# 64-wide turns by identity products become 128-wide transposes in a chunked recurrence, its outputs are formed beside its states, and attention scores use all 128 rows

## The chip, the cores and the metric

The kernel runs on one core of a Trainium2 chip. TensorE (PE in the rows) multiplies and transposes into eight PSUM banks of 128 x 512 f32; VectorE (DVE) and ScalarE (ACT) read the banks; GpSimd (POOL) does a few small things; loads are issued on the sync engine's queue (SP). The metric is device time of one execution in microseconds, lower is better.

## What is computed

Two transformer-like blocks over 512 tokens of width 1024. The change touches the first block's recurrence and the scores of the attention in both blocks.

```python
def rwkv7_step(state, inp):                       # 8 heads of 64, 512 steps
    r_t, w_t, k_t, v_t, a_t, b_t = inp
    sa = jnp.einsum('bhij,bhj->bhi', state, a_t)
    state = state * w_t[:, :, None, :] + sa[..., None] * b_t[:, :, None, :] + v_t[..., None] * k_t[:, :, None, :]
    y = jnp.einsum('bhij,bhj->bhi', state, r_t)
    return state, y
...
    y = yc * lax.rsqrt(jnp.mean(yc * yc, axis=-1, keepdims=True) + GN_EPS)
    y = y.reshape(b_, s_, D_RWKV) * lnx_g.astype(f32) + lnx_b.astype(f32)
...
    s = jnp.einsum('bhnqd,bhnkd->bhnqk', qc, kb).astype(jnp.float32) * (HEAD_DIM ** -0.5)   # band attention, 8 heads
...
        s = jnp.einsum('bhqd,bhkd->bhqk', qi, kh).astype(f32) * scale                       # second block, 4 heads
```

The first block projects the normalized input, runs the recurrence (512 channels) and a banded attention (512 channels), gates both and projects back. The second block has a state-space mixer, a second attention and a convolution side by side, and then 32 experts of which each token uses two. All in f32; large products are split into a high and a low part in f32r (one pass on TensorE), small ones are f32 (two passes).

## The kernel before

**Tiling of the recurrence.** Channels lie on partitions, so two heads of 64 fill 128 partitions (`HS` are the two halves), and there are four head pairs. The 512 steps are cut into chunks of 64; `rwkv_unit` treats one pair and one half of the sequence, four chunks (`NC = 4`), so there are 8 units. Two lanes of two pairs each run interleaved, with the attention (`att_stream`) and the modulation products (`ada_stream`) beside them.

**A unit, in order.** `pz` and `pa` are two small projections. `AR` holds the scaled a and r vectors, `BK` the scaled b and k. `psc` multiplies BK by AR for each chunk and head, masked into `SB[h]`. Then come the turns, which bring tokens to the partitions: `ptk` (BK into `SB[h][:, :, 128:192]`, by transposes of 64 rows), `pat` (the a part of AR into `RH`) and `pvt` (v into `UV`), both by products with the identity, 64 x 64, for each chunk and head, followed by one copy for each head. `pav` multiplies SB by UV. A triangular inverse of 32-wide blocks follows (`pf`, `p1`, `p2`), then `pwu`, `pgq` (into `Gb` and `Qb`) and `ph` (state parts `H_`). The state chain runs over the chunks (`px`, one product and one vector operation at a time). Then `py` forms the outputs: for each chunk `Qb` times the state, and SB times UV for each head, on the same bank. They are normalized over the head, turned back (`pyt`, again by identity products), scaled by `lnx_g` and `lnx_b`, and gated into `y`.

**Scores.** `score_parts` splits q and k: `Q[h]` holds the high part of q on one half of the partitions and the low part on the other, `K[h]` the high part of k twice, and `L` the low part of k. `scores` adds two f32r products on one bank: one with 128 rows, and one with 64 rows for L. It is called 32 times in the first block and 16 times in the second.

**What sets the order.** Nothing is issued as it is written. A recorder notes all operations; a planner (`schedule`, `cost`, `best`) then chooses, by a list of priorities and its own costs, an order for each engine, the PSUM bank of each tile and, for operations that are offered in two forms (`flex`, `copy`), ACT or DVE. It charges 130 ns when TensorE's tile shape changes and prefers to stay with a shape; all products on one PSUM tile keep their written order. `arrange` places the SBUF tiles. The order is then emitted and each engine follows its own list. All instructions are emitted from one line of the file (965), so the rows are told apart by shape.

Of the kernel before, what the change touches and what calls it, by code (L numbers as in the profile page):

```python
# [1012 lines left out]
def trace(R, T, off, dbg=None, stop=None):  # L1013
# [3 lines left out]
    C = {}  # L1017
# [216 lines left out]
    def rps(name):  # L1234
        return mmps(name, "rw", 4)
# [26 lines left out]
    def halves(name):  # L1262

        return rps(name + "0"), rps(name + "1")

    HS = (slice(0, 64), slice(64, 128))
    view = lambda p, n: p[:, :NC * n].rearrange("p (c n) -> p c n", n=n)

    def rwkv_unit(lane, pr, half, kx, kk, vx, rx, gx, st_):
# [34 lines left out]
        R.vector.scalar_tensor_tensor(ath, ath, 1.0, kk, ALU.add, ALU.mult)  # L1304
        AR = t512("AR")
        R.vector.scalar_tensor_tensor(AR[:, :, 0:64], kk, -1.0, E[:, :, 0:64], ALU.mult, ALU.mult)
        R.tt(AR[:, :, 64:128], rx, E[:, :, 1:65], ALU.mult)
        BK = t512("BK")
# [7 lines left out]
        for c in range(NC):  # L1316
            for h, hs in enumerate(HS):
                mm(ps_[h][:, 128 * c:128 * c + 128], lhsT=BK[hs, c], rhs=AR[hs, c], start=True, stop=True)
        SB = (t768("SB0"), t768("SB1"))
# [8 lines left out]
        yield  # L1328
        pt = halves("ptk")
        for c in range(NC):  # L1330
            for h, hs in enumerate(HS):
                R.tensor.transpose(pt[h][:, 64 * c:64 * c + 64], BK[hs, c], C["ident"][hs, hs])
        for h in range(2):
            R.copy(SB[h][:, :, 128:192], view(pt[h], 64))
        R32 = t256("R32")
# [5 lines left out]
        RH = t512("RH")  # L1341
        pt = halves("pat")
        for c in range(NC):
            for h, hs in enumerate(HS):
                mm(pt[h][hs, 64 * c:64 * c + 64], lhsT=AR[hs, c, 0:64], rhs=C["ident"][hs, hs], start=True, stop=True)
        for h, hs in enumerate(HS):
            R.copy(RH[hs, :, 0:64], view(pt[h], 64)[hs])
        UV = t512("UV").rearrange("p c (h n) -> p c h n", h=2)
        yield
        pt = halves("pvt")  # L1350
        for c in range(NC):
            for h, hs in enumerate(HS):
                mm(pt[h][HS[1 - h], 64 * c:64 * c + 64], lhsT=vx[hs, c], rhs=C["ident"][hs, hs], start=True, stop=True)
        for h in range(2):
            R.copy(UV[HS[1 - h], :, h], view(pt[h], 64)[HS[1 - h]])
        yield
# [68 lines left out]
        for h, hs in enumerate(HS):  # L1425
            pv = view(pt[h], 128)[hs]
            R.tt(Gb[hs, :, hs], pv[:, :, 64:128], i2b[hs], ALU.add)
            R.tt(Qb[hs, :, hs], pv[:, :, 0:64], AR[hs, :, 64:128], ALU.add)
        H_ = t256("H")
        p = view(rps("ph"), 64)  # L1430
        for c in range(NC):
            for h, hs in enumerate(HS):
                mm(p[hs, c], lhsT=SB[h][:, c, 128:192], rhs=UV[:, c, h], start=True, stop=True, tile_position=(0, 64 * h))
        R.tt(H_, p, D.unsqueeze(2).to_broadcast([128, NC, 64]), ALU.mult)
# [20 lines left out]
        st_.append(S2)  # L1455
        Y = view(rps("py"), 64)
        for c in range(NC):
            mm(Y[:, c], lhsT=Qb[:, c], rhs=X[:, c], start=True, stop=False)
            for h, hs in enumerate(HS):
                mm(Y[hs, c], lhsT=SB[h][:, c, 64:128], rhs=UV[:, c, h], start=False, stop=True, tile_position=(0, 64 * h))  # L1460

# [23 lines left out]
        yield  # L1485
        pt = halves("pyt")
        yn = t256("yn")
        for c in range(NC):
            for h, hs in enumerate(HS):
                mm(pt[h][hs, 64 * c:64 * c + 64], lhsT=Yc[hs, c], rhs=C["ident"][hs, hs], start=True, stop=True)  # L1490
        for h, hs in enumerate(HS):
            R.vector.tensor_scalar(yn[hs], view(pt[h], 64)[hs], Pc["lnx_g"][hs, c1], Pc["lnx_b"][hs, c1], ALU.mult, ALU.add)
        R.tt(yn, yn, bo, ALU.add)
# [37 lines left out]
    def qk_norm(j, g, name):  # L1531
# [11 lines left out]
        return o  # L1543

    def score_parts(q, k):

        Q, K = ([R.tile([128, 512], F32R, name) for _ in range(2)] for name in ("qs", "ks"))
        L = R.tile([128, 512], F32R, "kl")
        for h, hs in enumerate(HS):
            o = HS[1 - h]  # L1550
            R.copy(Q[h][hs], q[hs])
            R.tt(Q[h][o], q[hs], Q[h][hs].bitcast(F32), ALU.subtract)
            R.copy(K[h][hs], k[hs])
            R.copy(K[h][o], k[hs])
            R.tt(L[hs], k[hs], K[h][hs].bitcast(F32), ALU.subtract)
        return Q, K, L

    def scores(parts, h, qt, n):
        Q, K, L = parts
        ts = slice(128 * qt, 128 * qt + 128)  # L1560
        S = mmps("S")[:, :n]
        R.tensor.matmul(S, lhsT=Q[h][:, ts], rhs=K[h][:, :n], start=True, stop=False)
        R.tensor.matmul(S, lhsT=Q[h][HS[h], ts], rhs=L[HS[h], :n], start=False, stop=True)
        return S
# [1002 lines left out]
```

## Time and profile before

| what | value |
|---|---|
| median of 3 runs | 1463.89 us (1462.17 to 1464.84) |
| the profiled execution | 1457.32 us |
| its span, from first to last instruction | 1455.5 us |
| mean granted TensorE clock | 0.957 |

In the rows below, times are microseconds unless marked ns. The forms are rows*columns of the weights, then the moving operand. PE times are of matmul instructions, whose ends are modelled: the step from one start to the next is a measurement, a busy time less so. An f32 product is two matmul instructions, a transpose or an f32r product one.

### The profile page before, as it was taken

The page shows a single profiled execution, that of the slowest core. Times are in us where ns is not written, and L with a number is a line of the kernel's source. Part 1 is how long each engine was busy: PE and PEld are TensorE (multiplying, and loading weights), DVE is VectorE, ACT ScalarE, POOL GpSimd, SP SyncE. Part 2 cuts the span into 40 slices and gives each one's busy share as a digit, 9 for nine tenths or more (in the row PEclk, how much of TensorE's full clock was granted, in tenths as well). Part 3 has the DMA queues.
Part 4 walks back from the last instruction along what each step waited for, and adds up shares of the span by engine and source line. Part 5 has one row for each costly group of instructions (what it writes and reads, how often), then busy time and mean ns, then how long its engine had stood idle before and what let it go on. Part 6 is the DMA issues. An engine that isn't in the chain of part 4 may idle for free. (4 is left out here: it accounts for less than half of the span.)

```text
span 1455.5 us, 21894 instructions
## 1 busy us (share of the span) xinstructions
PE 1364.7 (94%) x7796; PEld 948.7 (65%) x7796; DVE 1204.1 (83%) x2196; ACT 814.0 (56%) x1250; POOL 167.7 (12%) x125
## 2 busy tenths in 40 slices
PE   5999999998999999999999899999999999989993
PEld 2766666666667787878789666666665565555562
DVE  5595882678796756799975889999999999999985
ACT  5463342455553335346652477877776676657762
POOL 0000000000010000000010213111132011151103
PEclk8999999999988998999999799999999999999997
DMA  9727377010011722000163489999999999999955
GB/s 333 295 93 260 139 238 283 30 38 23 31 44 52 247 81 70 15 30 1 58 232 130 158 297 341 364 368 364 348 362 352 351 344 361 349 337 313 359 188 180
DMA packets 90741, 307.78 MB, mean 211 GB/s; under 512 B 12034, under 2 KB 15490, under 8 KB 89604
## 3 DMA queue, kind: packets, MB, share of 16 engines
q1 hardware_dynamic: 85252, 293.75, 56.3%
q0 software_dynamic: 5376, 12.59, 2.5%
q8 instruction: 62, 1.02, 0.3%
q14 instruction: 51, 0.42, 0.1%
HBM read 293.72 MB, written 18.87 MB: 215 GB/s over the span
## 5 line engine op out<-in xcount | busy, mean ns | idle before, releaser
L965 PE MATMUL ps<-arear 128*80 128x512 f32 (+3 forms) x4435 | 1065.6, 391 | 31.1 <-DVE arear L965 15.8
L965 PEld LDWEIGHTS ps<-arear 128*80 128x80 f32 (+1 forms) x4435 | 704.5, 172 | 325.9 <-DVE arear L965 38.1
L965 ACT ACTIVATE arear<-areaf 128x1024 fp32r<-128x1024 f32 (+5 forms) x536 | 494.2, 949 | 283.7 <-PE ps L965 217.9
L965 DVE TENSOR_TENSOR arear<-areaf,arear 128x1024 fp32r<-128x1024 f32 (+5 forms) x560 | 600.5, 1106 | 61.5 <-ACT arear L965 28.9
L965 PE MATMUL ps<-areaf 64*64 64x64 f32 (+17 forms) x3361 | 371.3, 311 | 37.6 <-DVE areaf L965 26.4
L965 PEld LDWEIGHTS ps<-areaf 128*128 128x128 f32 (+6 forms) x3361 | 256.9, 149 | 158.4 <-issue 56.3
L965 ACT ACTIVATE areaf<-areaf 128x512 f32<-128x512 f32 (+11 forms) x238 | 121.3, 526 | 143.6 <-DVE areaf L965 119.4
L965 ACT ACTIVATE areaf<-ps 128x256 f32<-128x256 f32 (+7 forms) x253 | 110.4, 449 | 136.6 <-PE ps L965 126.5
L957 POOL DMA_INDIRECT yscr<-areaf,areai x32 | 110.3, 3448 | 464.2 <-DVE areaf L965 437.2
L965 DVE TENSOR_TENSOR areaf<-ps,areaf 80x512 f32<-80x512 f32 (+6 forms) x244 | 123.4, 514 | 23.7 <-PE ps L965 22.3
L965 DVE SCALAR_TENSOR_TENSOR areaf<-areaf 128x512 f32<-128x512 f32 (+6 forms) x190 | 108.7, 599 | 23.4 <-ACT areaf L965 17.8
L965 DVE TENSOR_TENSOR areaf<-areaf 128x512 f32<-128x512 f32 (+11 forms) x234 | 100.7, 451 | 8.6 <-ACT areaf L965 4.8
L965 DVE SCALAR_TENSOR_TENSOR areaf<-ps,areaf 128x511 f32<-128x511 f32 (+9 forms) x120 | 57.7, 493 | 41.2 <-PE ps L965 38.6
L965 POOL MEMSET areaf<- 128x512 f32 (+10 forms) x52 | 16.7, 328 | 422.9 <-PE ps L965 178.4
L965 ACT ACTIVATE areaf<-ps,areaf 128x128 f32<-128x128 f32 (+2 forms) x88 | 43.9, 534 | 36.7 <-PE ps L965 30.5
L965 POOL TENSOR_TENSOR areaf<-areaf 128x4 f32<-128x4 f32 (+2 forms) x21 | 20.8, 993 | 359.3 <-DVE areaf L965 328.8
L965 DVE TENSOR_SCALAR areaf<-areaf 128x1 f32<-128x1 f32 (+11 forms) x194 | 46.7, 266 | 14.8 <-PE ps L965 13.3
L965 DVE SCALAR_TENSOR_TENSOR areaf<-areaf,ps 80x512 f32<-80x512 f32 (+1 forms) x72 | 48.7, 676 | 0.8 <-ACT areaf L965 0.7
L965 DVE CAST arear<-areaf 128x1024 fp32r<-128x1024 f32 (+4 forms) x63 | 37.1, 588 | 10.9 <-PE ps L965 10.5
L965 ACT ACT_TABLE_LOAD x35 | 44.9, 1283 | 1.3 <-PEq L2553 0.7
L965 DVE COPY areaf<-ps 32x128 f32<-32x128 f32 (+9 forms) x58 | 22.4, 390 | 20.4 <-ACT areaf L965 14.4
L965 ACT ACTIVATE arear<-ps 128x320 fp32r<-128x320 f32 (+1 forms) x35 | 14.5, 415 | 27.6 <-PE ps L965 27.5
(31 smaller groups left out, 187.9 us busy)
## 6 DMA issues: line engine op xcount, KB each, us to landing
areaf<-in_wx_dram SPq DMA_DIRECT2D x384, 512.0 KB, 5.5
areaf<-in_wada_dram SPq DMA_DIRECT2D x56, 512.0 KB, 5.0
areaf<-in_win_c_dram SPq DMA_DIRECT2D x43, 512.0 KB, 4.4
areaf<-in_wada_dram SPq DMA_DIRECT2D x8, 1024.0 KB, 8.3
areaf<-in_wout_dram SPq DMA_DIRECT2D x16, 512.0 KB, 4.5
areaf<-in_xt_dram SPq DMA_DIRECT2D x16, 256.0 KB, 2.9
yscr<-areaf SPq DMA_DIRECT2D x8, 512.0 KB, 9.4
areaf<-in_win_c_dram SPq DMA_DIRECT2D x24, 128.0 KB, 7.5
```

The source lines that it names most:

```text
L957: self.emitted[i] = self.nc.gpsimd.indirect_dma_start(un(a[0]), bass.IndirectOffsetOnAxis(ap=un(k["idx"]), axis=0), un(k["in_"]), None, bo ...
L965: self.emitted[i] = getattr(getattr(self.nc, eng), op)(*[un(v) for v in a], **{n: un(v) for n, v in k.items()})
```

## The change

It does five things. `pat`, `pvt` and `pyt` become `turned`: 128x128 transposes of two chunks and two heads at a time on one bank, then one copy for each head and each chunk of the two, half of them from one half of the partitions to the other. `ptk` becomes four 128x128 transposes. AR holds its two parts one after the other. The products of SB and UV for the outputs stand beside those for the states, on a bank that the products with Qb are added to after the state chain; the scaling by `lnx_g` and `lnx_b` may go to ACT or DVE, from columns that are also kept with halves exchanged. In the scores, L becomes a tile for each head with zeros in its other half, so that its product has 128 rows.

```diff
--- before.py
+++ after.py
@@ -1265,6 +1265,24 @@
 
     HS = (slice(0, 64), slice(64, 128))
     view = lambda p, n: p[:, :NC * n].rearrange("p (c n) -> p c n", n=n)
+    chunks = lambda t: t.rearrange("p (q g) n -> p q g n", g=2)
+
+
+    lnx = [[Pc[n] for n in ("lnx_g", "lnx_b")], []]
+    for v in lnx[0]:
+        o = R.tile([128, 4], F32, "lnx")
+        for h in range(2):
+            R.copy(o[HS[1 - h]], v[HS[h]])
+        lnx[1].append(o)
+
+    def turned(name, src):
+
+
+        p = rps(name)
+        for q in range(NC // 2):
+            R.tensor.transpose(p[:, 128 * q:128 * q + 128], src[:, 2 * q:2 * q + 2].rearrange("p c n -> p (c n)"), C["ident"])
+        v = p[:, 0:64 * NC].rearrange("p (q h n) -> p q h n", h=2, n=64)
+        return [(h, g, v[HS[g], :, h]) for h in range(2) for g in range(2)]
 
     def rwkv_unit(lane, pr, half, kx, kk, vx, rx, gx, st_):
         t128, t256, t512, t768, ept = lane
@@ -1302,9 +1320,9 @@
         R.vector.tensor_scalar(k2, ath, hka[:, c1], oka[:, c1], ALU.mult, ALU.add)
         R.tt(k2, kx, k2, ALU.mult)
         R.vector.scalar_tensor_tensor(ath, ath, 1.0, kk, ALU.add, ALU.mult)
-        AR = t512("AR")
-        R.vector.scalar_tensor_tensor(AR[:, :, 0:64], kk, -1.0, E[:, :, 0:64], ALU.mult, ALU.mult)
-        R.tt(AR[:, :, 64:128], rx, E[:, :, 1:65], ALU.mult)
+        AR = t512("AR").rearrange("p c (h n) -> p (c h n)", h=2).rearrange("p (h c n) -> p h c n", h=2, n=64)
+        R.vector.scalar_tensor_tensor(AR[:, 0], kk, -1.0, E[:, :, 0:64], ALU.mult, ALU.mult)
+        R.tt(AR[:, 1], rx, E[:, :, 1:65], ALU.mult)
         BK = t512("BK")
         for h, hs in enumerate(HS):
             bs, ks = (HS[h], HS[1 - h])
@@ -1315,7 +1333,7 @@
         ps_ = halves("psc")
         for c in range(NC):
             for h, hs in enumerate(HS):
-                mm(ps_[h][:, 128 * c:128 * c + 128], lhsT=BK[hs, c], rhs=AR[hs, c], start=True, stop=True)
+                mm(ps_[h][:, 128 * c:128 * c + 128], lhsT=BK[hs, c], rhs=AR[hs, :, c], start=True, stop=True)
         SB = (t768("SB0"), t768("SB1"))
         msk = C["m2s"].unsqueeze(1).to_broadcast([128, NC, 128])
         ABc = t128("ABc")
@@ -1326,12 +1344,11 @@
                 R.copy(ABc[q], pv[q, :, 32 * b:32 * b + 32])
             R.tt(SB[h][:, :, 0:128], pv, msk, ALU.mult)
         yield
-        pt = halves("ptk")
+        pt = rps("ptk")
         for c in range(NC):
-            for h, hs in enumerate(HS):
-                R.tensor.transpose(pt[h][:, 64 * c:64 * c + 64], BK[hs, c], C["ident"][hs, hs])
-        for h in range(2):
-            R.copy(SB[h][:, :, 128:192], view(pt[h], 64))
+            R.tensor.transpose(pt[:, 128 * c:128 * c + 128], BK[:, c], C["ident"])
+        for h, hs in enumerate(HS):
+            R.copy(SB[h][:, :, 128:192], view(pt, 128)[:, :, hs])
         R32 = t256("R32")
         R.gpsimd.memset(R32, 0.0)
         for h in range(2):
@@ -1339,20 +1356,12 @@
             R.copy(R32[q, :, 32 * h:32 * h + 32], SB[h][q, :, 32:64])
         yield
         RH = t512("RH")
-        pt = halves("pat")
-        for c in range(NC):
-            for h, hs in enumerate(HS):
-                mm(pt[h][hs, 64 * c:64 * c + 64], lhsT=AR[hs, c, 0:64], rhs=C["ident"][hs, hs], start=True, stop=True)
-        for h, hs in enumerate(HS):
-            R.copy(RH[hs, :, 0:64], view(pt[h], 64)[hs])
+        for h, g, p in turned("pat", AR[:, 0]):
+            R.copy(chunks(RH)[HS[h], :, g, 0:64], p)
         UV = t512("UV").rearrange("p c (h n) -> p c h n", h=2)
         yield
-        pt = halves("pvt")
-        for c in range(NC):
-            for h, hs in enumerate(HS):
-                mm(pt[h][HS[1 - h], 64 * c:64 * c + 64], lhsT=vx[hs, c], rhs=C["ident"][hs, hs], start=True, stop=True)
-        for h in range(2):
-            R.copy(UV[HS[1 - h], :, h], view(pt[h], 64)[HS[1 - h]])
+        for h, g, p in turned("pvt", vx):
+            R.copy(UV.rearrange("p (q g) h n -> p q g h n", g=2)[HS[1 - h], :, g, h], p)
         yield
         pt = halves("pav")
         for c in range(NC):
@@ -1425,12 +1434,14 @@
         for h, hs in enumerate(HS):
             pv = view(pt[h], 128)[hs]
             R.tt(Gb[hs, :, hs], pv[:, :, 64:128], i2b[hs], ALU.add)
-            R.tt(Qb[hs, :, hs], pv[:, :, 0:64], AR[hs, :, 64:128], ALU.add)
+            R.tt(Qb[hs, :, hs], pv[:, :, 0:64], AR[hs, 1], ALU.add)
         H_ = t256("H")
         p = view(rps("ph"), 64)
-        for c in range(NC):
-            for h, hs in enumerate(HS):
-                mm(p[hs, c], lhsT=SB[h][:, c, 128:192], rhs=UV[:, c, h], start=True, stop=True, tile_position=(0, 64 * h))
+        Y = view(rps("py"), 64)
+        for o, whole, w in ((p, True, slice(128, 192)), (Y, False, slice(64, 128))):
+            for c in range(NC):
+                for h, hs in enumerate(HS):
+                    mm(o[hs, c], lhsT=SB[h][:, c, w], rhs=UV[:, c, h], start=whole or c == 0, stop=whole, tile_position=(0, 64 * h))
         R.tt(H_, p, D.unsqueeze(2).to_broadcast([128, NC, 64]), ALU.mult)
         yield
 
@@ -1453,11 +1464,8 @@
             R.vector.scalar_tensor_tensor(o, pt[:, :64], D[:, c:c + 1], H_[:, c], ALU.mult, ALU.add)
             yield
         st_.append(S2)
-        Y = view(rps("py"), 64)
         for c in range(NC):
-            mm(Y[:, c], lhsT=Qb[:, c], rhs=X[:, c], start=True, stop=False)
-            for h, hs in enumerate(HS):
-                mm(Y[hs, c], lhsT=SB[h][:, c, 64:128], rhs=UV[:, c, h], start=False, stop=True, tile_position=(0, 64 * h))
+            mm(Y[:, c], lhsT=Qb[:, c], rhs=X[:, c], start=False, stop=(c == NC - 1))
 
         mu_ = R.tile([128, NC], F32, "gmu")
         R.vector.tensor_reduce(mu_, Y, AX.X, ALU.add)
@@ -1483,13 +1491,12 @@
         R.scalar.activation(gth, gx, AF.Tanh, scale=0.5)
         R.vector.scalar_tensor_tensor(gth, gth, 1.0, gx, ALU.add, ALU.mult)
         yield
-        pt = halves("pyt")
         yn = t256("yn")
-        for c in range(NC):
-            for h, hs in enumerate(HS):
-                mm(pt[h][hs, 64 * c:64 * c + 64], lhsT=Yc[hs, c], rhs=C["ident"][hs, hs], start=True, stop=True)
-        for h, hs in enumerate(HS):
-            R.vector.tensor_scalar(yn[hs], view(pt[h], 64)[hs], Pc["lnx_g"][hs, c1], Pc["lnx_b"][hs, c1], ALU.mult, ALU.add)
+        for h, g, p in turned("pyt", Yc):
+            lg_, lb_ = (lnx[g != h][n][HS[g], c1] for n in range(2))
+            o = chunks(yn)[HS[h], :, g]
+            R.flex(("scalar", "activation", (o, p, AF.Identity), {"scale": lg_, "bias": lb_}),
+                   ("vector", "tensor_scalar", (o, p, lg_, lb_, ALU.mult, ALU.add), {}))
         R.tt(yn, yn, bo, ALU.add)
         R.vector.scalar_tensor_tensor(v3(y[pr][:, ts]), yn, 0.5, gth, ALU.mult, ALU.mult)
 
@@ -1542,17 +1549,20 @@
         R.vector.scalar_tensor_tensor(o, o, g, sq, ALU.mult, ALU.mult)
         return o
 
+    none = R.tile([128, 512], F32, "none")
+    R.gpsimd.memset(none, 0.0)
+
     def score_parts(q, k):
 
-        Q, K = ([R.tile([128, 512], F32R, name) for _ in range(2)] for name in ("qs", "ks"))
-        L = R.tile([128, 512], F32R, "kl")
+        Q, K, L = ([R.tile([128, 512], F32R, name) for _ in range(2)] for name in ("qs", "ks", "kl"))
         for h, hs in enumerate(HS):
             o = HS[1 - h]
             R.copy(Q[h][hs], q[hs])
             R.tt(Q[h][o], q[hs], Q[h][hs].bitcast(F32), ALU.subtract)
             R.copy(K[h][hs], k[hs])
             R.copy(K[h][o], k[hs])
-            R.tt(L[hs], k[hs], K[h][hs].bitcast(F32), ALU.subtract)
+            R.tt(L[h][hs], k[hs], K[h][hs].bitcast(F32), ALU.subtract)
+            R.copy(L[h][o], none[o])
         return Q, K, L
 
     def scores(parts, h, qt, n):
@@ -1560,7 +1570,7 @@
         ts = slice(128 * qt, 128 * qt + 128)
         S = mmps("S")[:, :n]
         R.tensor.matmul(S, lhsT=Q[h][:, ts], rhs=K[h][:, :n], start=True, stop=False)
-        R.tensor.matmul(S, lhsT=Q[h][HS[h], ts], rhs=L[HS[h], :n], start=False, stop=True)
+        R.tensor.matmul(S, lhsT=Q[h][:, ts], rhs=L[h][:, :n], start=False, stop=True)
         return S
 
     def softmax(S, n, bias):
```

## Rows read from the trace of the kernel before

**Rows 1.** The page: busy time, share and instructions; granted clock in 40 slices.
```profile
PE 1364.7 (94%) x7796; PEld 948.7 (65%) x7796; DVE 1204.1 (83%) x2196; ACT 814.0 (56%) x1250; POOL 167.7 (12%) x125
...
PEclk8999999999988998999999799999999999999997
```

**Rows 2.** Stretches: length, busy time of PE, PEld, DVE, ACT, POOL, clock, DMA, GB/s.
```profile
60.00:220.00 160.00, 157.84 (x1295) 102.49 (x1294) 126.67 (x327) 75.07 (x144) 6.21 (x13) 1.00 0.53 179
220.00:300.00 80.00, 80.00 (x464) 55.38 (x464) 36.53 (x82) 23.72 (x41) 3.04 (x7) 0.96 0.37 136
300.00:500.00 200.00, 188.92 (x1506) 134.75 (x1506) 165.74 (x465) 101.59 (x217) 12.15 (x26) 0.91 0.21 66
...
680.00:740.00 60.00, 58.69 (x389) 48.35 (x389) 59.48 (x184) 42.31 (x111) 4.74 (x5) 1.00 0.27 88
...
860.00:1400.00 540.00, 518.15 (x2260) 322.00 (x2259) 526.64 (x571) 383.83 (x432) 107.71 (x30) 0.99 0.96 350
```

**Rows 3.** Waits of PE from 60 to 500 us: total, times, longest.
```profile
PE ps L965 <- DVE areaf L965: 9.2, 19, 1.6
```

**Rows 4.** Timeline of PE at 580 us: start, length, instructions merged.
```profile
579.64 20.75 PE L965 MATMUL ps<-arear 128*128 128x512 f32 x89
```

**Rows 5.** PE instructions by form, 60 to 510 us: count, busy, mean ns, idle before.
```profile
L965 PE MATMUL ps<-areaf 64*64 64x64 f32 x512 | 33.6, 231 | 1.2 <-DVE areaf L965 1.1
...
L965 PE MATMUL ps<-areaf 64*128 64x64 f32 x64 | 7.6, 252 | 0.6 <-ACT areaf L965 0.5 <-DVE areaf L965 0.2
```

**Rows 6.** Timeline of PE around half a turn that stands alone.
```profile
491.63 0.47 PE L965 MATMUL ps<-arear 128*128 128x512 f32 x1
492.03 0.68 PE L965 MATMUL ps<-areaf 64*64 64x64 f32 x8
492.64 0.50 PE L965 MATMUL ps<-arear 128*128 128x512 f32 x1
```

**Rows 7.** Timeline of PE: 128x128 f32 passes between f32r ones; then one alone.
```profile
165.69 0.77 PE L965 MATMUL ps<-areaf 128*128 128x128 f32 x6
166.26 0.71 PE L965 MATMUL ps<-arear 128*128 128x512 f32 x2
166.81 0.27 PE L965 MATMUL ps<-areaf 128*128 128x128 f32 x1
```

**Rows 8.** Timeline of PE: state products; later, a chunk of the outputs.
```profile
208.33 0.69 PE L965 MATMUL ps<-areaf 128*64 128x64 f32 x16
208.95 0.73 PE L965 MATMUL ps<-arear 128*128 128x512 f32 x2
...
294.94 0.70 PE L965 MATMUL ps<-areaf 128*64 128x64 f32 x6
295.45 0.71 PE L965 MATMUL ps<-arear 128*128 128x512 f32 x2
```

**Rows 9.** Timeline of PE: both products of one score, and what follows.
```profile
719.20 0.91 PE L965 MATMUL ps<-arear 128*128 128x512 f32 x2
720.03 1.97 PE L965 MATMUL ps<-areaf 128*128 128x64 f32 x12
```

**Rows 10.** DVE and ACT instructions by form, 60 to 510 us.
```profile
L965 DVE TENSOR_SCALAR areaf<-ps,areaf 64x256 f32<-64x256 f32 x16 | 8.6, 538 | 0.4
L965 DVE COPY areaf<-ps 64x256 f32<-64x256 f32 x10 | 4.2, 420 | 3.8 <-ACT areaf L965 3.4 <-PE ps L965 0.2
...
L965 ACT ACTIVATE areaf<-ps 64x256 f32<-64x256 f32 x54 | 20.4, 377 | 41.9 <-PE ps L965 39.9 <-DVE areaf L965 1.5
L965 ACT ACTIVATE arear<-areaf 64x512 fp32r<-64x512 f32 x15 | 9.4, 629 | 10.5 <-DVE areaf L965 6.1 <-PE ps L965 4.1
L965 ACT ACTIVATE areaf<-ps 32x128 f32<-32x128 f32 x25 | 6.7, 267 | 12.4 <-PE ps L965 10.5 <-DVE areaf L965 1.6
```

**Rows 11.** Stretches of 20 us with a lower granted clock (the share before DMA).
```profile
420.00:440.00 20.00, 18.50 (x134) 12.85 (x136) 17.91 (x46) 9.73 (x19) 1.53 (x2) 0.66 0.05 13
...
460.00:480.00 20.00, 19.65 (x121) 15.31 (x120) 8.74 (x27) 4.00 (x10) 0.00 (x0) 0.66 0.32 106
```

## The prediction, made before the changed kernel was run

> **What bounds the kernel now.** The page comes first: TensorE (PE) is busy for 94% of the span and VectorE (DVE) for 83% [rows 1]. That average covers stages with different limits, so the table of stretches is next [rows 2]. The recurrence, the attention beside it and the modulation products run between about 60 and 500 us (the 64-wide products that only the recurrence issues all lie there). In that stretch PE is busy 157.84 of 160, 80 of 80 and 188.92 of 200 us, DVE 126.67, 36.53 and 165.74. In the second block's attention, 680 to 740 us, DVE is busy 59.48 of 60. In the expert stage, 860 to 1400 us, the DMA engines are busy 96% of the time at 350 GB/s: nothing of the change lies there, and it can only start earlier or later. So a microsecond cut from PE between 60 and 500 us should come off the end, as far as PE is what that stretch waits for.
>
> Is it? The view of waits says yes: in 440 us PE waited longest, in total, for DVE, and only 9.2 us [rows 3]. But the end of a matmul is modelled, so "busy" holds lost time too. The step from one start to the next shows it. At full clock, 512-column passes follow each other at 20.75/89, some 0.23 us [rows 4]. Whatever takes longer than its columns need is where the change can earn. I read those steps in the order of time (timeline).
>
> **The change, part by part.**
>
> *Turns.* Per unit (there are 8: four head pairs, two halves) the products by the identity for pat, pvt and pyt go, 8 each. An f32 product is two passes, so 48 passes of 64x64 go, and 8 transposes of 64 rows (ptk). In come 2+2+2+4 = 10 transposes of 128x128. The 64x64 form has 512 passes with 33.6 us busy; a quarter of them is pav, which stays, so 25.2 us go, and 7.6 us of ptk [rows 5]. Two corrections. A lone half turn of 8 passes reads 0.68 us but the next pass starts after 0.61, so busy overstates by 0.07 per block; and the pass before it took 0.40 instead of 0.23 until the turn began, so entering another tile shape costs 0.17 [rows 6]. With 32 blocks (8 x 4): 32.8 - 2.2 + 5.4 = 36 us if each is entered alone, 31 if none is. The trace has no row that singles out a 128-wide transpose fed from a recurrence tile. The nearest is a run of six 128x128 f32 passes that took 0.57 us to the next start, 0.095 each [rows 7]; from above, the 0.27 us that one such pass is busy in full. So 80 transposes cost 8 to 22 us. I take 8, since they can queue among f32r passes of the same shape. Removed: 31 to 36; net between 9 and 28, and I take 25, near the upper end, as each block was found entered more often than not.
>
> *Outputs beside states.* Y was, for each of 4 chunks, two passes of 128x128 (Qb) and then four of 128x64, all on one bank and thus in that order. One such alternation reads six passes in 0.51 us, plus 0.17 to enter [rows 8]: 0.68 x 4 x 8 = 22 us if each stands alone. After it, the 128x64 passes join those of ph: 16 passes took 0.62 us [rows 8], and 8 passes of Qb at 0.095 need 0.76, so 1.4 x 8 = 11. Between 0 (where chunks were already adjacent) and 11; I take 6. It also moves 16 passes off the end of the state chain; that is worth nothing by itself, for the chain has other work under it. The price is a PSUM bank held from ph to the end of the chain. In exchange ptk, pat, pvt and pyt need one bank where they needed two. I count it as nothing; if a bank were missing, PE would wait for the chain.
>
> *Scores.* The second product had 64 rows, another tile shape. First and second, both of 512 columns, took 0.83 us instead of 2 x 0.23 [rows 9]: 0.37 lost, 48 times, 18 us if each stood alone. Scores of neighbouring heads often stand together, which halves it: 9. Of the 48, 16 lie in the second block's attention, where DVE is full [rows 2]; there PE's gain is worth nothing. That leaves 6; bounds 3 and 12.
>
> *Added on ACT and DVE.* Each turn for pat and pvt is four copies of 64x128 instead of two of 64x256. A 64x256 copy takes 420 ns on DVE and 377 on ACT; the small end is 267 for 32x128 on ACT [rows 10], so the four take about 4 x 270 against 2 x 400: 0.3 us more, 16 times, 5 us. For pyt, two scalings of 538 ns on DVE [rows 10] become four that may also go to ACT. At between 267 and 538 each (I take 340): 0.3 us more, 8 times, 2 us. The zero halves of L are 12 copies of 64x512 at 629 ns [rows 10], or 7.5 us. In sum some 15 us over two engines. ACT is busy for 56% of the span [rows 1], so it is not on the path unless DVE is. The layout of AR and the four lnx copies change nothing that I can price: as many elements as before, and the lnx copies are done once.
>
> **Sum.** PE between 60 and 500 us gets 25 + 6 + 6 = 37 us less work. Does all of it pass? From 60 to 300 us DVE is busy 163 of 240 [rows 2]; half the units lie there, and I let nearly all of 18 us pass: 17. From 300 to 500 us DVE is already at 165.74 of 200. Less PE work would make that 166 plus some 4 of 182, or 93%; engines that feed each other in a fixed order don't both run at that. I let somewhat over half pass: 11. Together 28. The profiled execution took 1457.3 us (span 1455.5), so 1429; the median of the runs shown is 6.6 us above it, so **1436 us**.
>
> The order is made anew by the planner from its own costs, which no row prices: I widen by 8 us either way for it.
>
> **Clock.** The granted clock is 1.00 over most of the recurrence but 0.66 at 420 to 440 and at 460 to 480 us [rows 11]: two thirds of each at the lower of the two levels, 1.2 GHz. The stretches from 60 to 500 us average 0.95 [rows 2]. I forecast no change in it.
> The Trainium skill speaks against the change here ("TensorE: Matmul & The Clock Gate", Part 4: PE-mode transpose): a transpose is said not to count as work for the clock as a product does. No row of this trace stands apart enough to show it. By the skill the sum would lose clock where turns lie close together; by the rows, 80 transposes are at most 8 us of 440 and can't carry the clock either way.
>
> **Rivals.**
> 1. *DVE becomes the bound* in all of the recurrence, 60 to 220 us too, where it is at 79%. For: 93% needed later; more copies on the way from a turn to the next product. Against: DVE is light from 220 to 300 us, and pyt's scalings may go to ACT. About 12 us pass: 1452.
> 2. *The clock falls* (the other side). Place: 300 to 500 us, with four units close together. It now averages 0.91, some 36 us at 1.2 GHz. If the whole stretch ran at 1.2 GHz, 164 more would; a pass there takes twice as long, though not all PE time is passes, so I charge a quarter: 41 us lost against 28 won. That gives 1476. It decides when the loss passes 31 us: by half-rate work, 62 us more at 1.2 GHz, or a mean below 0.88 from 60 to 500 us. Against: what is removed are the small passes that stand around the low stretches. The skill's rule above would be its cause.
> 3. *The change doesn't shorten anything*: the new order waits for copies where it waited for tile shapes, so that PE issues fewer passes in the same time. For: PE's 9.2 us of shown waits are a floor, as ends are modelled. Each of 24 turns would have to wait 1.2 us for two more copies; they take 0.27 each. 1464.
> 4. *More than the sum*: all 37 pass and the low stretches shrink as well, which gives back some 10 us (at most a third of the two slices of 20 us [rows 11]): 1417.
>
> **How the numbers follow.** Forecast (PE sets the pace, partly held by DVE): 0.60, its own range 1424 to 1448. Rival 1: 0.17. Rival 2: 0.10. Rival 3: 0.07. Rival 4: 0.06. A measurement of this kernel can tell about 0.2% (3 us) from no change. Faster: 0.60 + 0.17 + 0.06 = 0.83; within 0.2%: 0.07; slower: 0.10. The range runs from 1414 (all parts at their better ends, below rival 4) to 1462, which takes in rivals 1 and 4 and part of 3; rival 2 and the rest of 3 are left out.
>
> **What would show it.** The 64x64 form should fall from 512 passes to 128, the 64-row transposes and the 64-row f32r passes should be gone, and 80 transposes of 128x128 should be new at some 0.1 us a step. 128x64 passes should stand in longer runs. The last 64x64 product of the recurrence, and with it the second block and the expert stage, should come some 28 us earlier, and the expert stage should be as long as before. DVE's share from 300 to 500 us should rise. Wrong would be: the same passes gone, but PE's steps around the turns longer (rival 3); DVE above 95% while PE waits for it (rival 1); a mean clock under 0.88 (rival 2); or a gain that is lost again before 860 us.

## The result and the profile after

The changed kernel takes 1428.28 us, the median of 4 runs (1428.20 to 1430.42), against 1464.37 us (1462.17 to 1466.83) for the kernel before in the same comparison: a ratio of 0.9757, 95% interval 0.9738 to 0.9775, or 36 us less. The prediction said 1436. Its profiled execution took 1430.42 us (span 1428.6), so between the two profiled executions lie only 26.9 us: the kernel before was profiled near the fast end of its runs, and the offset of 6.6 us that the prediction carried over was not there after. In every comparison here, runs over 1.5% above the fastest of their kernel are left out (three of e12's ten, none of the others).

The page of the changed kernel, PE's busy time and the granted clock, to be held against [rows 1]:

```profile
PE 1329.8 (93%) x7428; PEld 928.8 (65%) x7428; DVE 1196.3 (84%) x2181; ACT 841.0 (59%) x1329; POOL 187.8 (13%) x126
...
PEclk9999999998999989999998699999999999999997
```

There are 368 matmul instructions fewer. The two digits of 8 that the clock showed between 400 and 473 us are gone; one stands now at 321 to 357 us. The stretches (columns as in [rows 2]), the third cut at 470 us, where the recurrence now ends:

```profile
60.00:220.00 160.00, 156.55 (x1193) 104.23 (x1191) 122.79 (x312) 80.05 (x169) 7.53 (x16) 1.00 0.52 184
220.00:300.00 80.00, 74.82 (x432) 47.37 (x431) 51.33 (x137) 38.98 (x66) 2.04 (x6) 0.94 0.40 132
300.00:470.00 170.00, 160.66 (x1242) 115.49 (x1243) 144.31 (x409) 99.64 (x222) 11.77 (x21) 0.97 0.20 63
...
830.00:1370.00 540.00, 516.98 (x2269) 321.92 (x2269) 528.07 (x573) 390.57 (x440) 126.53 (x30) 1.00 0.96 351
```

The expert stage is what it was: the DMA engines busy 96% at 351 GB/s. In the recurrence DVE is little fuller in the last part (144.31 of 170 us, 85%; before 165.74 of 200, 83%) but more so from 220 to 300 us, where 36.53 us [rows 2] became 51.33. By form, PE from 60 to 480 us (count, busy, mean ns, idle before):

```profile
L965 PE MATMUL ps<-areaf 128*128 128x128 f32 x292 | 56.2, 286 | 7.9 <-DVE areaf L965 6.1 <-ACT areaf L965 1.4
...
L965 PE MATMUL ps<-areaf 128*64 128x64 f32 x256 | 12.8, 230 | 0.9 <-ACT areaf L965 0.9
L965 PE MATMUL ps<-areaf 64*64 64x64 f32 x128 | 8.6, 225 | 0.5 <-DVE areaf L965 0.5
```

64x64 passes went from 512 to 128, and the 64-row transposes of [rows 5] are gone. The 128x64 passes, of which there are as many as before, are busy for 12.8 us (17.6 in e5 below, which has the old work). PE's waits from 60 to 470 us, 9.2 us in [rows 3], are a little more:

```profile
PE ps L965 <- DVE areaf L965: 13.8, 20, 2.6
PE ps L965 <- ACT areaf L965: 2.4, 3, 1.2
```

**Where the time came from.** The records of PE are in the order of PE's list, so each matmul can be given its product. The table sums the steps (a matmul's start to the next one's start) from 60 us to the last `pyt`; the sums of all products together are the length of the recurrence, so nothing is counted twice.

| steps, us | before | after | difference |
|---|---|---|---|
| end of the recurrence | 498.8 | 470.4 | -28.4 |
| turns (ptk, pat, pvt, pyt) | 30.9 (447 passes) | 8.7 (79) | -22.2 |
| outputs and state parts (py, ph) | 25.0 | 20.4 | -4.6 |
| scores in this stretch | 14.1 | 12.5 | -1.6 |
| all others | 368.8 | 368.8 | 0.0 |

(The last pass of `pyt` ends the stretch and is not in it.) The turns, the outputs and the scores make up the whole of the 28.4 us. The 79 transposes step at 0.11 us in the mean; here four of them, between passes of their tile shape, take 0.36, or 0.09 each:

```profile
84.01 0.60 PE L965 MATMUL ps<-areaf 128*128 128x128 f32 x4
84.37 0.47 PE L965 MATMUL ps<-arear 128*128 128x512 f32 x1
```

After the recurrence little changes: 332 us instead of 326 up to the first expert product (`pg`, each expert's first), and from the first `pg` to the last 584 instead of 588.

The "others" are not one thing, though. The clock's records give 41.0 us at 1.2 GHz in the recurrence before and 20.5 after. Had the passes issued at that level taken the mean of their product at full clock, they would have been 18.7 us shorter before and 9.8 after: by this estimate some 9 us of the 28.4 came with the clock, about 23 with the removed passes, and some 4 were given back in other steps that grew.

### The profile page after: what moved, and what is told of

Same layout as the page of the kernel before. It is cut to its first block, busy times and chain, and to the rows that moved or that the text cites. A ratio compares the mean times of both kernels' runs of the same rounds, so it can differ in the third digit from the quotient of the medians.

```text
span 1428.6 us, 21272 instructions
## 1 busy us (share of the span) xinstructions
PE 1329.8 (93%) x7428; PEld 928.8 (65%) x7428; DVE 1196.3 (84%) x2181; ACT 841.0 (59%) x1329; POOL 187.8 (13%) x126
## 5 line engine op out<-in xcount | busy, mean ns | idle before, releaser
L965 PE MATMUL ps<-arear 128*80 128x512 f32 (+4 forms) x4435 | 1061.9, 390 | 36.0 <-ACT arear L965 13.5
L965 ACT ACTIVATE arear<-areaf 128x1024 fp32r<-128x1024 f32 (+5 forms) x552 | 508.0, 944 | 277.6 <-PE ps L965 210.7
L965 PE MATMUL ps<-areaf 128*32 128x128 f32 (+16 forms) x2993 | 348.4, 316 | 40.8 <-DVE areaf L965 31.8
L965 PEld LDWEIGHTS ps<-areaf 128*128 128x128 f32 (+6 forms) x2993 | 241.7, 148 | 154.5 <-DVE areaf L965 58.3
L957 POOL DMA_INDIRECT yscr<-areaf,areai x32 | 129.6, 4050 | 439.5 <-DVE areaf L965 425.5
L965 ACT ACTIVATE areaf<-ps 128x512 f32<-128x512 f32 (+6 forms) x278 | 114.3, 425 | 123.8 <-PE ps L965 113.1
L965 DVE TENSOR_TENSOR areaf<-ps,areaf 128x512 f32<-128x512 f32 (+6 forms) x244 | 123.6, 515 | 19.3 <-PE ps L965 17.7
L965 DVE SCALAR_TENSOR_TENSOR areaf<-areaf 128x512 f32<-128x512 f32 (+7 forms) x190 | 108.8, 602 | 18.4 <-ACT areaf L965 14.4
L965 ACT ACTIVATE areaf<-ps,areaf 128x128 f32<-128x128 f32 (+3 forms) x111 | 54.1, 517 | 55.2 <-PE ps L965 51.5
L965 DVE COPY areaf<-ps 32x128 f32<-32x128 f32 (+7 forms) x65 | 23.3, 361 | 27.7 <-ACT areaf L965 15.2
```

The lines of the kernel that those rows point to most:

```text
L957: self.emitted[i] = self.nc.gpsimd.indirect_dma_start(un(a[0]), bass.IndirectOffsetOnAxis(ap=un(k["idx"]), axis=0), un(k["in_"]), None, bo ...
L965: self.emitted[i] = getattr(getattr(self.nc, eng), op)(*[un(v) for v in a], **{n: un(v) for n, v in k.items()})
```

## The experiments

Theory A is the prediction's: passes leave TensorE, which sets the pace. Theory B: the planner makes a new order for whatever work it gets, and the order is what moved the time. Theory C: the copies on DVE and ACT hold the path. The kernel before ran beside each group: 1462.56 us with the first four, 1462.19 with the next four, 1462.62 with the last.

**One part at a time, and none.** The first three take one part's hunks of the change each, with an order made anew: all of `turned`, `ptk` and `AR` (e1); the hunks at `ph` and `py` (e2); the hunks of the scores (e3). The fourth has the work of the kernel before and one constant of the planner changed, the limit in its list of priorities up to which it prefers to stay with a tile shape:

```diff
-TURN, STICK = 130, 800
+TURN, STICK = 130, 700
```

e1, the turns: 

> Only the turns (and the scaling after them) are changed; outputs and scores are as before. Theory A (PE work passes, by its terms): 25 us less PE work, of which three quarters pass: 19 us faster than before, 1445. Theory B (the gain is owed to how the new order happens to fall): any time between 1430 and 1465, with no relation to the work removed, and the three parts alone don't add up to 36 us. Theory C (DVE holds the recurrence): at most 10 us faster.

e2, the outputs: 

> Only the outputs stand beside the states; turns and scores are as before. Theory A: 6 us less PE work in changes of tile shape, 4 to 6 us faster, about 1459. Theory B: unrelated to the 6 us, between 10 us faster and 10 us slower. If the bank that is held through the state chain matters: slower than before, with PE waiting near the chain.

e3, the scores: 

> Only the scores use 128 rows; the rest is as before. Theory A: 6 us less PE work in the first block, nothing in the second (DVE is full there), 5 us faster, about 1459. If the second block's share passes too: 8 us faster. Theory B: unrelated, 10 us either way.

e4, no part: 

> The kernel before with one constant of the planner changed (a shape is kept up to 700 instead of 800 of its priority), so that the work is the same and the order another. Theory A: within 4 us of before. Theory B: up to 10 us away from it, which would be the size of chance in each of the other times.

| kernel | us | ratio (95%) | end of recurrence | first, last `pg` |
|---|---|---|---|---|
| before (profiled 1457.3) | 1462.56 | | 498.8 | 825.0, 1413.1 |
| changed (profiled 1430.4) | 1428.28 | 0.9757 (0.9738 to 0.9775) | 470.4 | 802.1, 1386.4 |
| e1 turns | 1477.44 | 1.0124 (1.0076 to 1.0172) | 479.3 | 833.6, 1436.2 |
| e2 outputs | 1488.41 | 1.0155 (1.0115 to 1.0195) | 532.6 | 864.7, 1447.3 |
| e3 scores | 1464.58 | 1.0018 (0.9994 to 1.0041) | 488.1 | 820.0, 1416.9 |
| e4 no part, new order | 1482.44 | 1.0142 (1.0113 to 1.0171) | 507.7 | 849.9, 1433.0 |

No part by itself is faster, and the same work in another order is 20 us slower (e4). A's times are missed in all four, and so are B's, but for e3: orders scatter more than either theory allowed. Taken as times, the parts say nothing. By place they do: with the turns alone the recurrence ends 19.5 us earlier, and the gain is lost afterwards (354 us to the first expert product instead of 326, 603 from the first `pg` to the last instead of 588). In e2 the recurrence itself grew by 34 us. Its stretch from 300 to 500 us, against [rows 2], and PE's longest kind of wait from 60 to 500 us, against [rows 3]:

```profile
300.00:500.00 200.00, 178.76 (x1353) 123.92 (x1353) 148.51 (x421) 89.22 (x193) 9.33 (x20) 0.85 0.13 41
```
```profile
PE ps L965 <- DVE areaf L965: 20.9, 25, 5.5
```

PE is idle more, waits for DVE, and the clock falls to 0.85: an order in which products stand before their operands are there. Whether the outputs or the order did that, these runs can't tell. So the next ones hold the order still.

**Parts put into the order of the kernel before.** The planner gets the work of the kernel before. Then each new operation is put where the one that it replaces stood, on each engine; only the PSUM banks are handed out anew. The core of it, from e6, with cuts marked by dots (`PLAN` names the changed parts in the work that the order is made for, `WORK` those in the work that is put into it; t are the turns, y the outputs):

```diff
+PLAN, WORK = "", "t"
...
+                FL.update(WORK)
+                W_, _ = record(None)
+                mine_ = W_.tags()
+                order, _, _ = W_.freeze(mine_, atp, engine, False)
...
+                order2, t0, bank = R.freeze([mine_[i] for i in order], at, engine, True)
```

e5: 

> The kernel before, with every engine's order kept; only the PSUM banks are handed out anew, in that order. It measures what the handing out of banks costs and is the control for the next three. Theory A (the change acts through TensorE's work) and theory B (through the order that the planner happens to make) both expect the time of the kernel before, 1462 us within 5.

e6: 

> The turns alone (pat, pvt, pyt and ptk as 128x128 transposes), put into the order of the kernel before: each new transpose and copy stands where the products and copies that it replaces stood. Theory A: 19 to 25 us below the control, about 1440, as the run with the turns alone and an order made anew had its recurrence end 19.5 us earlier. Theory B: within 6 us of the control, since no order has changed. A third, theory C (the copies hold the path): above the control by some 5 to 10 us, as 16 turns have two copies more.

e7: 

> Turns and outputs beside states, both put into the order of the kernel before. Theory A: 4 to 6 us below the run with the turns alone in this order, 23 to 31 below the control, about 1435. Theory B: within 6 us of the control. The outputs alone, with an order made anew, were 26 us slower than before; if that lay in the outputs themselves (a bank held from ph to the end of the state chain), this kernel is over 20 us slower than the one with the turns alone.

e8: 

> Outputs beside states alone, in the order of the kernel before; the work of the run that was 26 us slower when its order was made anew. Theory A: 4 to 6 us below the control, about 1457. Theory B: within 6 us of the control, and the 26 us are the order's. If the held bank is the cause of the 26 us, this kernel is over 20 us slower than the control.

| kernel, in the order of before | us | ratio (95%) | end of recurrence | steps of turns |
|---|---|---|---|---|
| e5 old work | 1458.35 | 0.9999 (0.9962 to 1.0035) | 495.9 | 31.5 |
| e6 turns | 1455.94 | 0.9963 (0.9936 to 0.9990) | 491.6 | 19.4 |
| e7 turns and outputs | 1449.78 | 0.9937 (0.9902 to 0.9971) | 489.3 | 19.8 |
| e8 outputs | 1455.30 | 0.9977 (0.9946 to 1.0007) | 492.3 | 33.4 |

The banks cost nothing (e5). The outputs are 3 us below that control at the medians (the intervals overlap) and end the recurrence 3.6 us earlier (e8); so the 26 us that e2 lost are its order's, and the held bank did no harm here. Turns and outputs together (e7) are 8.6 us below the control and end the recurrence 6.6 us earlier, far from A's 23 to 31. The turns alone give 2.4 us at the medians, 5 by the ratios (here too the intervals overlap), and 4.3 at the recurrence's end, not the 19 to 25 of theory A. Their steps shrink by 12 us only, to 0.25 us for a transpose, and the other steps grow by 8. A step lasts until the next matmul starts, so it holds the wait of the product behind it: of the 19.4 us of the turns, 6.7 are idle time before the next product. One place shows how. In e5 (first fence) 24 passes of pyt and pvt stand before the second product of a score; in e6 (second fence) 4 transposes stand there:

```profile
431.45 0.97 PE L1084 MATMUL ps<-areaf 64*64 64x64 f32 x24
432.73 0.75 PE L1084 MATMUL ps<-arear 64*128 64x128 f32 x2 [0.30 <-DVE arear L1084]
```
```profile
425.31 0.60 PE L1084 MATMUL ps<-areaf 128*128 128x128 f32 x4
427.73 0.99 PE L1084 MATMUL ps<-arear 64*128 64x128 f32 x3 [1.82 <-DVE arear L1084]
```

The passes went from 24 to 4, but the score's product needs what DVE writes, and PE follows its list: it waits 1.82 us where it waited 0.30, and the stretch takes 2.42 us instead of 1.28. PE's waits for DVE and ACT from 60 to 490 us, e5 first, then e6:

```profile
PE ps L1084 <- DVE areaf L1084: 10.0, 18, 2.0
PE ps L1084 <- ACT areaf L1084: 2.3, 3, 1.3
PE ps L1084 <- DVE arear L1084: 0.3, 1, 0.3
```
```profile
PE ps L1084 <- DVE areaf L1084: 13.4, 28, 1.4
PE ps L1084 <- ACT areaf L1084: 5.2, 5, 1.7
PE ps L1084 <- DVE arear L1084: 1.8, 1, 1.8
PE ps L1084 <- ACT arear L1084: 0.8, 1, 0.8
```

So theory A holds only with an addition, D: the removed passes pay in an order that fills the place they leave. A share of the added copies in these waits is not excluded: from 60 to 500 us ACT is busy for 218.9 us in e6 and 200.8 in e5 (DVE for 323.3 and 330.2), and no run has the transposes without the copies. The scores were not put into this order; that is left untried.

**The turns undone in the new order, and other orders.** e9 is the changed kernel with its own order, and the identity products and copies of 64 in the places of the transposes. e10 and e11 are the whole change with the planner's limit at 700 and 900, and e12 is the work of the kernel before with 900, as e4 is with 700.

```diff
+PLAN, WORK = "ty", "y"
```

e9: 

> The changed kernel with the turns alone undone, in the changed kernel's own order: the identity products and copies of 64 stand where the transposes and their copies stood. Theory A (the change acts through TensorE's work): the turns' steps grow from 8.7 us to the 31 us that they took before, and the time by 22 us to about 1450. Theory B (the order alone): within 6 us of the changed kernel's 1428. Theory D, which the fixed orders suggested (work that is put into an order made for other work loses more than it should): over 1460.

e10: 

> The whole change, its order made anew with the planner's limit for staying with a tile shape at 700 instead of 800; the kernel before with 700 took 1482 us. Theory A: about 28 us under that pair, 1454. Theory B: orders scatter by 20 us whatever the work, so anything between 1428 and 1490, with no tie to 1482.

e11: 

> The whole change with the limit at 900. Theory A: about 28 us under the kernel before with 900. Theory B: no such tie; over the three limits the mean of the changed kernels is within 10 us of the mean of the others.

e12: 

> The work of the kernel before with the limit at 900: the partner of the run before. Theory A: about 28 us above it. Theory B: between 1440 and 1490 with no tie to it.

| kernel | us | ratio (95%) | end of recurrence | first, last `pg` |
|---|---|---|---|---|
| e9 turns undone, order of the changed | 1455.99 | 0.9952 (0.9925 to 0.9980) | 494.0 | 823.5, 1411.0 |
| e10 whole change, 700 | 1434.09 | 0.9785 (0.9724 to 0.9846) | 473.4 | 804.5, 1391.0 |
| e11 whole change, 900 | 1466.11 | 1.0033 (0.9991 to 1.0075) | 470.2 | 820.4, 1415.9 |
| e12 old work, 900 | 1478.35 | 1.0116 (1.0076 to 1.0156) | | |

(e12's profiled execution took 1497.69, so its places are not given.) e9 is 27.7 us slower than the changed kernel: theory B would have had under 6, A 22, and D's time of over 1460 is not reached. The recurrence ends 23.6 us later, of which the steps of the turns, 24.2 instead of 8.7, are 15.5; the other 8 are other steps that grew. Doing the turns the old way in the new order thus costs 28 us, where doing them the new way in the old order gives 2 to 5. Both figures hold a loss from putting work into an order that was made for other work; in e6 it hides part of the gain, in e9 it adds to it. What the turns are worth by themselves lies between. The banks are handed out anew in e9 too; that this costs nothing was measured in the old order alone (e5).

At each limit the changed work beats the old: by 12 us at 900 (1466.11 and 1478.35), by 34 at 800 (1428.28 and 1462.6) and by 48 at 700 (1434.09 and 1482.44), 32 in the mean, where B had the means within 10 and A had 28 each time. The end of the recurrence is steady over the orders of the whole change, 470.2 to 473.4, and comes at 498.8 and 507.7 without it. The scatter comes later. e11 has the earliest end of all and loses it in the second block: 350 us to the first expert product instead of 332. DVE's waits from 480 to 820 us, two kinds of the changed kernel and then of e11, and DVE's timeline in e11:

```profile
DVE areaf L965 <- PE ps L965: 32.1, 21, 7.2
DVE areaf L965 <- ACT areaf L965: 7.9, 8, 2.5
```
```profile
DVE areaf L965 <- ACT areaf L965: 28.5, 12, 16.0
DVE areaf L965 <- PE ps L965: 20.0, 15, 4.4
```
```profile
542.79 1.23 DVE L965 TENSOR_TENSOR arear<-areaf,arear 128x1024 fp32r<-128x1024 f32 x1 [2.03 <-ACT arear L965]
559.98 0.69 DVE L965 SCALAR_TENSOR_TENSOR areaf<-areaf 128x512 f32<-128x512 f32 x1 [15.97 <-ACT areaf L965]
```

One DVE operation stands 16 us ahead of the ACT result that it needs, and DVE's list stops behind it. But ACT itself waits there, 16.1 us, for PE, and PE is full. The stretch from 540 to 560 us (columns as in [rows 2]), the changed kernel first, then e11:

```profile
540.00:560.00 20.00, 20.00 (x95) 16.55 (x94) 2.83 (x3) 3.94 (x6) 0.00 (x0) 1.00 0.09 27
```
```profile
540.00:560.00 20.00, 20.00 (x94) 16.42 (x93) 2.00 (x3) 2.43 (x4) 0.00 (x0) 1.00 0.00 0
```

DVE idles nearly as long in the changed kernel, in several shorter waits. So the longest wait is not by itself what e11 loses. From 480 to 640 us its DVE has done 8 us less (106.93 and 114.88 busy), and from 640 to 720 us DVE is full and PE is busy for 69.37 of 80 us (76.88 in the changed kernel). The kernel before has DVE as full there (79.71) with PE at 77.62, so a full DVE alone does not explain it either:

```profile
640.00:720.00 80.00, 69.37 (x425) 56.28 (x423) 79.11 (x214) 53.65 (x142) 4.17 (x5) 0.96 0.12 38
```

What costs e11 the 18 us in the second block stays open, as do the 11 us more from its first `pg` to the last (595.5 instead of 584.3).

## Why the prediction was right, and where it was not

**PE sets the pace, and the gain passes to the end: right.** The end of the recurrence moved by 28.4 us and the end of the span by 26.9. The prediction's 28 and its 1429 for the profiled execution (measured 1430.4) are met, but partly by errors that cancel, as follows; that the number came so close is in part luck.

**Turns, -25: measured -22.2 in steps.** The old turns took 30.9, the lower bound of the 31 to 36: few of them are entered alone. The 80 transposes took 8.7 where 8 was said. Both hold for an order made for them; in the old order the same transposes took 19.4, of which 6.7 are waits of the product behind, so that this is near the upper bound of 22 for another reason than the one given. The condition "since they can queue among f32r passes of the same shape" was the right one, and it was the planner that met it.

**Outputs, -6: -4.6. Scores, -6: -1.6** in the recurrence. The old scores stepped at 0.22 us a pass in the mean (14.1 over 64), half of what [rows 9] show for a pair that stands alone. That pair has 512 columns, though, and the scores of the first block have 128, 256, 384 and 512, a quarter each; at the 0.23 us of 512 columns [rows 4] and in proportion they would need some 9 us, an estimate, so that at most 5 were to be won. e3 gained 10.7 us by the recurrence's end and nothing in time; its score steps fell by 1.0 only (14.1 to 13.1), so the order did the rest.

**Added copies, some 15 us over DVE and ACT: right.** The forms of the changed kernel from 60 to 475 us, against [rows 10]:

```profile
L965 ACT ACTIVATE areaf<-ps 64x128 f32<-64x128 f32 x47 | 12.8, 272 | 18.8 <-PE ps L965 15.2 <-DVE areaf L965 3.1
L965 ACT ACTIVATE areaf<-ps 64x256 f32<-64x256 f32 x22 | 8.3, 377 | 8.6 <-PE ps L965 5.8 <-DVE areaf L965 2.7
L965 ACT ACTIVATE areaf<-ps,areaf 64x128 f32<-64x128 f32 x23 | 10.4, 454 | 3.2 <-DVE areaf L965 2.4 <-PE ps L965 0.5
...
L965 DVE COPY areaf<-ps 64x128 f32<-64x128 f32 x17 | 4.9, 289 | 3.7 <-ACT areaf L965 3.5
L965 DVE COPY areaf<-ps 64x256 f32<-64x256 f32 x10 | 4.2, 423 | 7.0 <-ACT areaf L965 5.0 <-PE ps L965 1.9
...
L965 DVE TENSOR_SCALAR areaf<-ps,areaf 64x128 f32<-64x128 f32 x9 | 3.7, 409 | 1.2 <-ACT areaf L965 0.9
```

The copies take 30.2 us instead of 24.6, the scalings 14.1 instead of 8.6 (23 of 32 went to ACT, at 454 ns where 340 was taken), and the copies and casts of 64x512 about 4 more. With all their other work DVE and ACT were busy 529.3 us from 60 to 500 us before (DVE 328.9, ACT 200.4) and 537.1 from 60 to 470 after (318.4 and 218.7): the added work went to ACT, which is off the path in the changed kernel's order, as said.

**28 of 37 pass: the step that failed first.** The sum was 28, not 37, and all of it passed in steps (by the estimate above, 23 less work and 9 from the clock, with 4 given back). DVE at 93% from 300 us on was the reason for the discount; it was 85%, as the new order has more of DVE's work in the stretch from 220 to 300 us, where it had slack. The sign that DVE's share from 300 to 500 us should rise did not come: 159.41 of 200 after 165.74. A discount for one stretch's share does not hold when the order is made anew over all of them.

**No change in the clock: off by some 9 us.** The mean from 60 us to the end of the recurrence rose from 0.95 to 0.98 (160 us at 1.00, 80 at 0.94, 170 at 0.97). It goes with the order, not with the turns: e9, with the old turns in the new order, had 24 us at 1.2 GHz, e3, with the old turns in a new order, 20.5, and e10 and e11 27 and 24, while e5 to e8 in the old order had 34 to 44 and e1, with the new turns in an order of its own, 44. So rival 2 was wrong, and the clock part of rival 4 came true. The Trainium skill's remark that a transpose doesn't count for the clock as a product does ("TensorE: Matmul & The Clock Gate", Part 4: PE-mode transpose) can't be read from these runs: e6, with 80 transposes in the old order, had 44 us at the low level beside e5's 38, too close to part, and the changed kernel 20.5.

The clock also bears on the 36 us between the medians. Over 73 executions of the kernel before, 1451 to 1471 us long, the mean clock ran from 0.965 down to 0.950, the longer ones mostly with the lower clock. The three at 0.964 and 0.965 took 1451.5 to 1454.4, and the changed kernel's execution at 0.964 took 1430.4. At the same clock the two kernels are thus some 21 to 24 us apart; the rest goes with the clock. Few executions show it, and they do not tell which is the cause.

**8 us either way for the order: the step that failed most.** Old work took 1462, 1482 and 1478 us in three orders, new work 1428, 1434 and 1466. A spread of 20 to 38 us is as large as the effect, and the range, up to 1462, held only because this change's order came out as good as the one before (e11, at 1466, lies outside it). What is settled: with the orders of three limits the change is worth 32 us in the mean, between 12 and 48, and undoing its largest part in its own order costs 28. What stays open is how much a fourth order would take back.

**Rivals 1 and 3** (DVE bounds, 1452; nothing shortened, 1464): the changed kernel refutes both, but each is to be seen elsewhere: rival 3 in e6, where PE waits for DVE and ACT in place of tile shapes, and a full DVE in the second block of e11. Theory C had e6 above its control by 5 to 10 us for its added copies; it was below.

## What to carry to other kernels

Where a planner orders the whole program, compare several orders of the old work before believing a few per cent, and read a part by its place in the trace (when does its stage end?), not by the total time. Work taken from the engine that sets the pace pays when the order fills the place that it leaves: the same turns gave 2 to 5 us in an order made for others, and undoing them in their own cost 28. Putting a part into the order of another kernel errs against the part that is put in, so do it both ways, with a control. And follow a long wait to its end before blaming it: the longest one of e11's DVE led through ACT to a TensorE that was full.

## What had not been expected of the hardware

128x128 transposes of f32 step at 0.11 us in the mean of the changed kernel (0.09 in the place shown), about as an f32 pass of that size in [rows 7] (0.095); in the old order they step at 0.25 in the mean (19.4 us for 79), or 0.16 without the idle time before the next product. Changes of the tile shape (rows or columns of 32, 64 or 128) in PE's list fell from 400 to 284 in the recurrence; at the 0.17 us of [rows 6] for each, an estimate, that is 20 of the 28 us. The price is rather an upper one: e7 has 312 changes where e5 has 400, 15 us by it, and ends the recurrence 6.6 us earlier. The Trainium skill says that a change of tiling mode drains TensorE ("TensorEngine Tiling (Array Packing)", Key Properties); the step of 0.40 us instead of 0.23 before such a change [rows 6] agrees. The time at 1.2 GHz in the recurrence followed the order of the work more than its kind: 20 to 27 us in three orders of the changed kernel, 34 to 44 in one order with four kinds of work, and from 20.5 (e3) to 82 (e2) in orders made anew for single parts.
